# A decoder block on eight cores: packing the scattered transposes, re-ordering the first loads and groups, and moving work off the Vector engine

## The chip, the cores and the metric

The kernel runs on all eight NeuronCores of one Trainium2 chip, one sequence of 2048 tokens on each core, and the cores do not exchange data. The metric is device time in microseconds (us) of the slowest core. Most executions of a kernel agree within 0.3%. Now and then one die (cores 0 to 3 or 4 to 7) runs at a lower granted TensorE clock and the time is longer; such slow runs are left out wherever two kernels are compared.

The engines are called PE (matrix multiply), DVE (Vector), ACT (Scalar), POOL (GpSimd) and SP (which here only issues transfers). PEld is PE's weight load. "The kernel before" and "the changed kernel" are the two sides of the change. In the profiles `L453` and the like are line numbers of the kernel at hand; most instructions are issued by small helpers, so a line stands for a kind of instruction and not for a place in the algorithm, and the two kernels number the same helper differently.

## The reference, cut to what matters

```python
h = rmsnorm(x, norm_mix_g[l])
proj = h @ w_in[l]
q_pre, k_pre, v, o_pre, i_pre, f_pre, conf_in, gate_pre = jnp.split(proj, SPLITS, axis=-1)
# ... mLSTM branch on q, k, v: the "mixer loop" below ...

# Conformer convolution branch: this is the stretch ahead of the mixer loop
a, ga = jnp.split(conf_in, 2, axis=-1)
u = a * jax.nn.sigmoid(ga)
u = causal_dwconv(u, conf_conv_w[l], conf_conv_b[l])      # 31 taps, 1024 channels
u = jax.nn.silu(layernorm(u, conf_ln_g[l], conf_ln_b[l]))

x = x + (g_m * branch_m + g_c * branch_c) @ w_out[l]      # the w_out stage
x = x + (silu(f @ w_ffn_gate[l]) * (f @ w_ffn_up[l])) @ w_ffn_down[l]   # FFN, then down
gate = sigmoid(rmsnorm(x, norm_ple_g[l]) @ w_ple_gate[l]) # PLE gate weights
x = x + gate * (p[l] @ w_ple_proj[l])
```

D_MODEL is 1024, the sequence is cut into four token blocks T of 512 tokens (`TT`), each of four tiles of 128, and the 1024 convolution channels into eight groups c of 128.

## The kernel before

A small scheduler takes a program of operations in priority order, simulates it, fixes an order for each engine and inserts the semaphore waits. All SBUF data lie in one tensor, `arena`; `V(offset, n, dtype)` is a view of it. The parts that the change touches:

```python
def norm_pre(j):                                   # one tile of 128 tokens
    rms(xin0[j % 6], hb0[j % 3], gmix)             # ACT square sum, POOL pow, DVE multiply
    if j + 4 < NTOK:
        xload(j + 4)

def A(c, T):                                       # one projection group: u = a * sigmoid(ga)
    w = Aw[c % 4]                                  # four weight sets
    bg, ba = ringA(), ringA()
    mmg(bank(bg), [(w[:, 1, kc, :], hT[:, kc, tsl(T)]) for kc in range(8)])
    th = thr_()
    act(th, bank(bg), AF.Tanh, scale=0.5)
    mmg(bank(ba), [(w[:, 0, kc, :], hT[:, kc, tsl(T)]) for kc in range(8)])
    u = ur()
    stt(u, th, 1.0, bank(ba), ALU.add, ALU.mult)
    vtr(utr[c % 4][:, :, 1 + 16 * T:17 + 16 * T].rearrange("p c b -> p b c"),
        u.rearrange("p (b t) -> p b t", t=32))     # DVE 32x32 transposes, scattered bf16 output

def expand(h):                                     # filters into a block-diagonal weight
    i, half = h // 2, h % 2
    for q in range(4):
        # ... cut: src, dst: 32 partitions x 1024 elements ...
        ts('dve', dst, src, 0.5, ALU.mult)

def conv_evac(i):                                  # four PSUM transposes a convolution
    for T in range(NT):
        src = ps[:, 0:2048].rearrange("p (c b) -> p b c", b=64)[:, 16 * T:16 * T + 16, :]
        vtr(uc(i, T).rearrange("p (b t) -> p b t", t=32), src)

def stats(i, T):                                   # sums for the layer norm
    k = s2()
    b = pcol[:, PC_CCB + i:PC_CCB + i + 1]
    ts('dve', ucb[k], uc(i, T), b, ALU.add)
    act(usq[k], uc(i, T), AF.Square, bias=b)
    # ... cut: two matmuls ...

def ln_apply(i, T, b0):
    u = uc(i, T)
    stt(u, u, pcol[:, PC_CCB + i:PC_CCB + i + 1], bank(b0), ALU.add, ALU.mult)
    tt('pool' if i % 4 else 'dve', u, u, mrs, ALU.subtract)
    # ... cut: Silu on ACT ...
```

The loads at the start are issued at once: four x tiles, the gain, then A weights, two filter groups and gate weights. The order of work ahead of the mixer loop is: four norms; for each T three groups A(0..2, T); then A(3..7, T) with one convolution after every third group. At the other end, the last piece of the down weights:

```python
for n, T in forder:                                # FFN
    F(n, T)
    # ... cut ...
    if n == 9:
        cast('pg0', V(PGo[0], 4 * D, BF16), din['wPG'][:, 0:4 * D])
    if n == 18:
        cast('pg1', V(PGo[1], 2 * D, BF16), din['wPG'][:, 4 * D:6 * D])
    if n == 19:
        cast('pg2', V(PGo[2], 2 * D, BF16), din['wPG'][:, 6 * D:8 * D])
cast('dw3', V(dwoff[3], 4 * D, BF16), din['wD'][:, 18 * D:22 * D])   # over the FFN's thF buffers
```

## Time and profile before

| | kernel before |
|---|---|
| median of the 4 first runs | 1443.31 us (1439.45 to 1672.77; the largest was slow) |
| profiled run, slowest core | 1444.3 us (core 2) |
| first projection matmul | 40.6 us |
| mixer loop at full PE use from | about 340 us |
| last FFN matmul to last store of y | about 1192 to 1442 us |

Most of the lines that matter are shown in the prediction. One view that it used in words only is the list of transfers of the first 80 us (destination and source, issuing queue, number, size, median us from issue to landing), of the kernel before:

```profile
arena<-x SPq DMA_DIRECT2D x16, 512.0 KB, 16.4
arena<-wA POOLq DMA_DIRECT2D x4, 512.0 KB, 17.2
arena<-wS POOLq DMA_DIRECT2D x2, 1024.0 KB, 41.0
```

One tile of x takes 16.4 us to land with everything in flight together, among it two 1 MB pieces of q/k weights (wS) that nothing needs before about 250 us.

### The profile page before, as it was taken

What the parts mean: (1) busy time and instruction counts of PE and PEld (TensorE: products, weight loads), DVE (VectorE), ACT (ScalarE), POOL (GpSimd) and SP (SyncE); (2) the same over time, 40 slices, a digit from 0 to 9 for tenths busy, and PEclk for the clock granted to TensorE, in tenths of its full rate; (3) what the DMA queues carried; (4) which work ended last, traced back from release to release, by engine and by line L of the source; (5) the groups of instructions that cost most, each with busy time, mean ns of one, the idle gap of its engine ahead of it and who ended that gap; (6) DMA issues with size and microseconds to landing.
All of it is one profiled execution on the core that took longest, in us unless ns stands there. A gap on an engine that the chain in (4) does not pass through costs nothing.

```text
span 1444.3 us, 20115 instructions; the slowest of 8 cores (1428.2 to 1444.3 us)
## 1 busy us (share of the span) xinstructions
PE 1293.6 (90%) x6921; PEld 619.9 (43%) x7048; DVE 756.7 (52%) x1218; ACT 496.9 (34%) x917; POOL 277.4 (19%) x423
## 2 busy tenths in 40 slices
PE   0588999847989999999999999999999997999997
PEld 0234444314544454544444444444444443444443
DVE  4687899788888888621122255212121211545444
ACT  2332224666666666321111145111111110333233
POOL 2000001274445444322112201000000000000000
PEclk9888999768999999999999999999999998999999
DMA  9703231020033002332312498822212203121211
GB/s 196 188 28 60 48 55 31 0 44 1 1 59 59 2 1 45 74 74 31 57 30 40 75 254 222 154 37 37 44 30 44 44 16 102 59 88 59 88 59 73
DMA packets 22131, 94.23 MB, mean 65 GB/s; under 512 B 2704, under 2 KB 2832, under 8 KB 18960
## 3 DMA queue, kind: packets, MB, share of 16 engines
q0 software_dynamic: 9504, 48.26, 20.7%
q1 hardware_dynamic: 12528, 44.69, 9.3%
q8 instruction: 58, 0.95, 0.3%
q14 instruction: 41, 0.34, 0.1%
HBM read 124.41 MB, written 16.78 MB: 98 GB/s over the span
## 4 chain that ended last, share of the span: by engine, by line
PE 76%; DVE 7%; DMA 6%; issue 6%; ACT 4%; POOL 1%; SPq 0%; DVEq 0%; ACTq 0%; POOLq 0%
PE ps L396 74%; DVE arena L449 4%; DMA arena<-x 4%; ACT arena L419 3%; PE ps L399 2%; DVE arena L441 2%; DVE arena L446 1%; DMA arena<-wD 1%; ACT arena L435 1%; DMA x1d<-arena 1%; POOL arena L446 1%; DVE arena L453 0%; POOL arena L437 0%; SPq L84 0%; POOL arena L441 0%
## 5 line engine op out<-in xcount | busy, mean ns | idle before, releaser
L396 PE MATMUL ps<-arena 128*128 128x512 bf16 (+4 forms) x6281 | 1264.2, 357 | 74.9 <-ACT arena L419 23.4
L396 PEld LDWEIGHTS ps<-arena 128*128 128x128 bf16 (+1 forms) x6408 | 576.6, 99 | 720.8 <-issue 136.0
L419 ACT ACTIVATE arena<-ps 128x512 f32<-128x512 f32 (+3 forms) x414 | 217.4, 532 | 598.5 <-PE ps L396 580.6
L449 DVE SCALAR_TENSOR_TENSOR arena<-arena 128x512 f32<-128x512 bf16 (+3 forms) x353 | 278.0, 809 | 33.0 <-POOL arena L446 13.4
L449 DVE SCALAR_TENSOR_TENSOR arena<-arena,ps 128x512 f32<-128x512 f32 (+2 forms) x216 | 151.5, 709 | 211.7 <-PE ps L396 204.6
L446 POOL TENSOR_TENSOR arena<-arena 128x1 f32<-128x1 f32 (+3 forms) x152 | 139.7, 924 | 554.0 <-DVE arena L441 350.6
L419 ACT ACTIVATE arena<-arena 128x512 bf16<-128x512 f32 (+3 forms) x199 | 157.1, 800 | 244.1 <-DVE arena L446 95.5
L446 DVE TENSOR_TENSOR arena<-arena,ps 128x512 bf16<-128x512 f32 x88 | 60.5, 688 | 237.5 <-PE ps L396 235.9
L399 PE MATMUL ps<-arena 128*128 128x128 bf16 x640 | 60.5, 229 | 66.7 <-DVE arena L449 44.4
L399 PEld LDWEIGHTS ps<-arena 128*128 128x128 bf16 x640 | 47.3, 102 | 94.0 <-issue 76.6
L449 DVE SCALAR_TENSOR_TENSOR arena<-ps,arena 128x128 bf16<-128x128 f32 (+2 forms) x160 | 70.0, 466 | 32.2 <-DMA arena<-x 17.1
L435 ACT COPY arena<-ps 128x1024 bf16<-128x1024 bf16 (+1 forms) x72 | 59.0, 820 | 79.9 <-PE ps L399 79.5
L441 DVE TENSOR_SCALAR arena<-arena 32x1024 bf16<-32x1024 bf16 (+4 forms) x165 | 53.1, 327 | 57.8 <-ACT arena L419 55.8
L453 DVE STREAM_TRANSPOSE arena<-arena 128x512 bf16<-128x512 bf16 x32 | 78.7, 2458 | 1.3
L446 DVE TENSOR_TENSOR arena<-ps,arena 128x512 f32<-128x512 f32 (+2 forms) x34 | 23.1, 679 | 88.5 <-PE ps L396 85.3
L441 POOL TENSOR_SCALAR arena<-arena 128x514 bf16<-128x514 f32 (+1 forms) x61 | 54.0, 886 | 76.7 <-DVE arena L449 56.0
L437 POOL COPY arena<-arena 128x3 bf16<-128x3 bf16 x128 | 47.7, 375 | 106.3 <-ACT arena L419 64.4
L84 POOL DMA_DIRECT2D arena<-wF x22 | 11.8, 535 | 233.3 <-PE ps L396 233.3
L419 ACT ACTIVATE arena<-ps,arena 128x512 f32<-128x512 f32 x64 | 50.0, 783 | 0.0
L446 DVE TENSOR_TENSOR arena<-arena 128x2 f32<-128x2 f32 (+3 forms) x47 | 22.7, 492 | 15.7 <-ACT arena L419 15.6
L453 DVE STREAM_TRANSPOSE arena<-ps 128x512 f32<-128x512 f32 x32 | 23.6, 739 | 0.1
L435 ACT CAST arena<-ps 128x512 bf16<-128x512 f32 x32 | 18.8, 589 | 13.6 <-PE ps L396 12.4
(26 smaller groups left out, 104.6 us busy)
## 6 DMA issues: line engine op xcount, KB each, us to landing
arena<-x SPq DMA_DIRECT2D x32, 512.0 KB, 7.8
arena<-wF POOLq DMA_DIRECT2D x22, 512.0 KB, 5.3
arena<-wS POOLq DMA_DIRECT2D x8, 1024.0 KB, 10.0
arena<-wM POOLq DMA_DIRECT2D x8, 1024.0 KB, 10.3
x1d<-arena SPq DMA_DIRECT2D x16, 512.0 KB, 4.9
arena<-x1d SPq DMA_DIRECT2D x16, 512.0 KB, 4.3
y<-arena SPq DMA_DIRECT2D x16, 512.0 KB, 2.9
arena<-wD POOLq DMA_DIRECT2D x3, 1536.0 KB, 15.3
```

What stands on the lines that cost most here:

```text
L84: n.subs = [(lambda g: g.dma_start(out=out, in_=in_), [self.region(in_)], [self.region(out)])]
L396: S.op('pe', lambda e: e.matmul(out, lhsT=lhsT, rhs=rhs, start=start, stop=stop), [lhsT, rhs], [out], c)
L399: S.op('pe', lambda e: e.transpose(out=out, in_=in_, identity=identb), [in_, identb], [out], 0.06)
L419: S.op('act', lambda e: e.activation(out=out, in_=in_, func=func, **kw), [in_] + aps(bias, scale), [out] + aps(accum), c)
L435: S.op('act', lambda g: g.copy(out=out, in_=in_), [in_], [out], c)
L437: S.op(e, lambda g: g.tensor_copy(out=out, in_=in_), [in_], [out], c)
L441: S.op(e, lambda g: g.tensor_scalar(out=out, in0=in_, scalar1=s1, scalar2=s2, op0=op0, **kw), [in_] + aps(s1, s2), [out], vcost(e, out, [i ...
L446: S.op(e, lambda g: g.tensor_tensor(out=out, in0=a, in1=b, op=op), [a, b], [out], c)
L449: S.op('dve', lambda g: g.scalar_tensor_tensor(out=out, in0=a, scalar=s, in1=b, op0=op0, op1=op1), [a, b] + aps(s), [out], vcost('dve', ou ...
L453: S.op('dve', lambda g: g.transpose(out=out, in_=in_), [in_], [out], 0.19 + nfree(in_) * (1.0 if in_.dtype == F32 else 4.4) / 1e3)
```

## The change

The intent is to let PE start sooner and to take work off DVE in the stretch where both are full. It has seven parts: (1) u of T and T+2 are interleaved, so that one f32 transpose carries two bf16 values; (2) three of four filter expansions go to POOL; (3) the bias additions of the statistics go to ACT; (4) half of the layer-norm subtractions read the mean from PSUM on DVE, the other half stay on POOL; (5) x tiles, A weights and filters are one stream in order of need with at most three transfers in flight; (6) token block 0 is projected tile by tile, there are six A weight sets, and 24 of 32 groups run before the first convolution, in the order T = 0, 2, 1, 3 that the packing wants; (7) the last down weights load early and half of the PLE gate weights load late. The core of the diff:

```diff
+        TORD = (0, 2, 1, 3)
+        tiles = [4 * T + j for T in TORD for j in range(4)]
+        def stream(q, k, out, in_):
+            n = landed[0]
+            landed[0] += 1
+            dma(q, k, out, in_, dw=['st%d' % n], dr=['st%d' % (n - 3)] if n >= 3 else [])
 ...
-        def A(c, T):
-            w = Aw[c % 4]
+        def A(c, T, split=False):
+            w = Aw[c % 6]
+            u = uT[c if c < 6 else 2 * (c % 2) + T % 2]
 ...
+                if split:
+                    for j in range(4):
+                        mmg(bank(b, 128 * j, 128 * j + 128), [(w[:, m, kc, :], hT[:, kc, js(4 * T + j)]) for kc in range(8)])
 ...
-            stt(u, th, 1.0, bank(ba), ALU.add, ALU.mult)
-            vtr(utr[c % 4][:, :, 1 + 16 * T:17 + 16 * T].rearrange("p c b -> p b c"), u.rearrange("p (b t) -> p b t", t=32))
+            stt(u[:, T // 2::2], th, 1.0, bank(banks[1]), ALU.add, ALU.mult)
+            if T >= 2:
+                h = T % 2
+                vtr(utr4[c % 6][:, :, 1 + 16 * h:17 + 16 * h].rearrange("p c b -> p b c"), u.bitcast(F32).rearrange("p (b t) -> p b t", t=32), 4.6)
+                if h == 1:
+                    copy('dve', utr[c % 6][:, :, 0, 1], utr[c % 6][:, :, 32, 0])
 ...
-                ts('dve', dst, src, 0.5, ALU.mult)
+                if q == 0:
+                    ts('dve', dst, src, 0.5, ALU.mult)
+                else:
+                    ts('pool', dst, src, 0.5, ALU.mult, 1.0, ALU.mult)
 ...
-            ts('dve', ucb[k], uc(i, T), b, ALU.add)
+            act(ucb[k], uc(i, T), AF.Identity, bias=b)
 ...
-            tt('pool' if i % 4 else 'dve', u, u, mrs, ALU.subtract)
+            if i % 2:
+                tt('pool', u, u, mrs[T % 2], ALU.subtract)
+            else:
+                tt('dve', u, u, bank(b1), ALU.subtract)
 ...
                 if n == 9:
-                    cast('pg0', V(PGo[0], 4 * D, BF16), din['wPG'][:, 0:4 * D])
+                    cast('dw3', V(dwoff[3], 4 * D, BF16), din['wD'][:, 18 * D:22 * D])
 ...
-        cast('dw3', V(dwoff[3], 4 * D, BF16), din['wD'][:, 18 * D:22 * D])
+        cast('pg2', V(PGo[2], 4 * D, BF16), din['wPG'][:, 4 * D:8 * D])
```

Cut: the new buffer addresses, the scheduler's extra cost for table loads, a rule by which POOL waits for itself when it changes to other partitions, the new loops over groups and convolutions.

## The prediction

> **What bounds the kernel now.** I first read the fast runs (1445.6, 1441.0 and 1439.5 us; 1672.8 is the slow state) and the cores: 1428 to 1444 us, the two dies within 1%, so one core stands for all. Then the engines in nine stretches of the slowest core (length; busy us of PE, PEld, DVE, ACT, POOL; granted clock; DMA share; GB/s):
>
> ```profile
> 0.00:40.00 40.00, 5.06 (x40) 3.87 (x40) 19.18 (x23) 9.62 (x15) 9.67 (x29) 1.00 0.97 196
> 40.00:80.00 40.00, 24.48 (x114) 11.54 (x117) 25.31 (x33) 12.66 (x21) 3.74 (x7) 0.79 0.67 176
> 80.00:120.00 40.00, 32.86 (x168) 15.58 (x171) 32.33 (x31) 11.53 (x19) 4.35 (x8) 0.91 0.13 21
> 120.00:260.00 140.00, 128.54 (x1089) 62.12 (x1099) 127.51 (x191) 48.95 (x78) 8.56 (x23) 0.95 0.26 44
> 260.00:340.00 80.00, 46.88 (x163) 19.23 (x164) 64.33 (x90) 51.29 (x84) 45.25 (x46) 0.66 0.10 20
> 340.00:600.00 260.00, 240.88 (x1435) 128.47 (x1464) 226.11 (x456) 163.79 (x376) 115.42 (x189) 1.00 0.20 33
> 600.00:1190.00 590.00, 582.67 (x2781) 270.35 (x2836) 154.25 (x239) 128.17 (x217) 72.27 (x91) 1.00 0.36 73
> 1190.00:1210.00 20.00, 9.41 (x37) 3.90 (x37) 1.38 (x2) 0.60 (x1) 0.53 (x1) 0.73 0.72 184
> ```
>
> The kernel is PE-bound from 340 us on (PE 93 to 99%). The losses lie ahead of that: 50 us of idle PE in the first 80, 18 in 80 to 260, 33 in 260 to 340, and 10.6 at 1190. In 80 to 260 both PE and DVE are near full, so there no engine alone can give much. The pieces of the chain that ended last, from two stretches of it, name the two DMA waits (start, us, what):
>
> ```profile
> 5.23 32.98 DMA arena<-x
> ...
> 1193.50 13.31 DMA arena<-wD
> ```
>
> The first is x arriving beside everything else that was issued at the start; the first projection matmul runs at 40.6 us. The second is the last piece of the down weights, which overwrites a buffer that the FFN uses to its end. Who fills DVE in 80 to 260, by shape:
>
> ```profile
> L453 DVE STREAM_TRANSPOSE arena<-arena 128x512 bf16<-128x512 bf16 x29 | 71.3, 2457 | 1.0
> L453 DVE STREAM_TRANSPOSE arena<-ps 128x512 f32<-128x512 f32 x32 | 23.6, 739 | 0.1
> L441 DVE TENSOR_SCALAR arena<-arena 32x1024 bf16<-32x1024 bf16 x52 | 22.1, 425 | 0.7
> L449 DVE SCALAR_TENSOR_TENSOR arena<-arena,ps 128x512 bf16<-128x512 f32 x28 | 19.1, 681 | 12.1 <-PE ps L396 11.9
> L441 DVE TENSOR_SCALAR arena<-arena 128x512 bf16<-128x512 f32 x32 | 15.5, 492 | 0.7 <-PE ps L396 0.7
> ```
>
> The bf16 transposes alone are 71 of 160 busy us. In the layer-norm stretch, the timeline of DVE has this (start, us, instructions):
>
> ```profile
> 305.21 7.67 DVE L446 TENSOR_TENSOR arena<-arena 128x512 f32<-128x512 f32 x2
> ```
>
> Two subtractions of 0.69 us each (as at 275.57) take 3.8 us each while POOL does the same subtractions; PE idles meanwhile.
>
> [...]the transpose that scatters bf16 with a 130-byte step takes 2457 ns for 512 elements, the one with a dense output 739 ns.[...] the trace has 8 loads of 1283 ns, all before 340 us and mostly off the path.
>
> **The change part by part.**
> 1. Transposes: 32 bf16 ones become 16 f32 ones, each carrying tile T and T+2 interleaved. Same 512 elements, same scatter, so I keep 2.46 us each: 78.7 to 39.3 us, DVE -39.4. ([...]the multiply now writes bf16 with a step of two[...], so I leave it at 0.68.)
> 2. Filter expansion: 64 of 427 ns on DVE; 48 go to POOL. DVE -20.5. On POOL a one-input scale of 1024 elements took 1.04 us, so +50 us, plus waits on itself where the partition window changes.
> 3. Statistics: 32 bias additions of 492 ns go to ACT, at about the 0.74 us of the Square of that shape. DVE -15.5, ACT +24.
> 4. Layer norm: 24 subtractions on POOL (1.42 us) become 16; 8 on DVE (1.88 us[...]) become 16 from PSUM (0.69): 14.8 to 11.0 on DVE, about -11 on POOL.
> Sum on DVE: -39.4 - 20.5 - 15.5 - 3.8 = -79 us of the 269 it does before 340 us.
> 5. Loads: x and the A weights come as one stream in order of need, at most three in flight; filters and q/k weights wait. Up to the last x tile that is 8.4 MB of x, 0.5 of the gain, 3.1 of weights as stored, 12 MB; at the 176 to 196 GB/s above, 61 to 68 us, so x ends near 70 us, as it about does now. What is gained is the first tile: four transfers of 0.26 to 0.5 MB share the pipe, x lands near 7 us, and the norm chain (1.06 + 0.18 + 0.15 + 0.55 + 1.28, PE transposes 1.0, copy 0.7 to 1.0, hops) ends near 14 us.
> 6. Splitting tile 0 into 128-column matmuls lets PE start on one token tile. It is nearly free: 8 such transposes took 0.45 us in the chain, 56 ns each, 4 x 56 = 224 ns against about 216 for one 512-column matmul.
> 7. Order: six A weight sets and u-buffers instead of four; 24 of 32 A groups run before the first convolution; the transposes no longer stand just ahead of each convolution.
> 8. The last down weights load early, into space of their own; the late load is half of the PLE gate weights, of 1 MB, which took 13.3 us for the down piece and is needed only about 19 us after the down stage starts (its first gate matmuls come after two down tiles). I count the 10.5 us as gained.
>
> **Adding up the stages.** PE work at full clock: an A group is 16 x 0.216 = 3.46 us[...].
> - First: 24 groups and 128 transposes, 83 + 7 = 90 us, at the clock of about 0.9 seen from 80 to 120, 100 us: 14 to 114. DVE needs about 85 in it and x has landed by 70, so PE sets it.
> - Second: 8 groups 27.7,[...] statistics 48 x 0.216 = 10.4, gates 4: 66, with clock and hand-offs (a convolution waits for four PSUM transposes of 0.74 before it) 74: to 188. DVE needs 44, ACT about 45, POOL 37 to 45.
> - Third: two convolutions, four q/k groups, the rest of the statistics: PE 18, ACT 20, DVE 16; 22: to 210.
> - Fourth: the layer norm, where PE waits on DVE. DVE had 64 busy of 80; now 60, with the 16 of idling cut to about 7: 67, to 277.
> The same point is now reached at 340, so -63; with the down weights -11: 1443 - 74 = 1369.
>
> **The rivals.** (a) PE alone bounds all of it from 14 us on: its 239 busy us before 340, some at a low clock, are about 222 at full; the point would be reached near 240, the kernel at 1335. For it: 79 us off DVE. Against: the norm still needs over 40 us of DVE after the last statistics. (b) POOL becomes the bound of the convolutions: three expansions a half are 3.2 us by row, but if partition-window waits[...] make it 2 us each, 6 us a half, 96 us for 16 halves, more than the 74 + 22 of stages two and three, and the kernel would lose 10 to 25 of the gain: 1380 to 1395. For it: POOL also issues the filter loads in the same order, behind waits. (c) The stream starves: three in flight with a round of waits between, at say 130 GB/s, x would end near 95 us and stage one near 125, +10 to 15. (d) f32 scatter costs more than bf16 scatter, say 4 us: +24 us of DVE, but half of that lies where PE sets the pace: +10. (e) The freed time returns as waits in the mixer loop at 340 to 600, where DVE has 226 of 260: the loop is unchanged, so I give this little.
>
> **Range and chances.** The gain has four parts of about 27 (start), 15 (80 to 260), 20 (norm) and 11. Rivals b, c, d together take perhaps 30 and a adds 35. I put 1368 in the middle and 1338 to 1400 for 8 in 10. Within 2% begins at 1414, which needs two rivals at once: 0.06; faster 0.93; slower 0.01.
>
> **What would show it.** First projection matmul near 14 us (10 to 18) instead of 40.6; x waits in the chain short. Scattered transposes: 16 of about 2.5 us. DVE busy up to the mixer loop about 190 us. The mixer loop's first full-PE stretch near 277 us instead of 340. POOL expansions near 1.05 us. Subtractions on DVE at 0.69 us. No wait on down weights and none over 3 us on the gate weights. Wrong would be: PE idle under POOL in the convolutions, a granted clock still near 0.7 in the norm with idle as before, or a difference after 340 us other than the 11.

The sum came to 74 us: 63 ahead of the mixer loop and 11 in the tail. A term within it is cut above: 23.4 us for six convolutions, part of the 66 of the second stage (two more convolutions are in the 18 of PE of the third). It rested on a rate for narrow matmuls that no trace shows; in the kernel before, 64 matmuls of 64 columns, one convolution, take PE 2.1 to 2.5 us of busy time. The 0.216 us of a 512-column matmul is in the chain of the kernel before (32 in 6.92 us from 47.01). That an f32 element of the scatter costs what a bf16 one does (2.46 us for 512), that the interleaved multiply stays at 0.68 us, and that subtractions from PSUM take 0.69 us beside POOL's were estimates from the times above.

## The result, and the profile after

The changed kernel took 1378.27 us in the median of ten runs (fast ones 1376.96 to 1381.05, their mean 1378.4); the kernel before, with more runs beside it, 1444.91 us in the median of sixteen. The ratio of the two is 0.953, with a 95% interval of 0.9495 to 0.9566. Ratios are the mean time of one kernel's fast runs over that of the other's of the same rounds, so not quite the ratio of these medians. The profiled executions are 1444.3 and 1377.7 us: 66.6 us less, where 75 were predicted. Seven of the sixteen runs of the kernel before are slow ones or ones of 1456 to 1462 us; the other nine have a mean of 1442.4 us, and against them the gain is 64 us.

The engines of the changed kernel in stretches of time (length; busy us of PE, PEld, DVE, ACT, POOL; granted clock; DMA share; GB/s). The first four are those of the same view before; the mixer loop, which began at 340, now begins near 291, so the next stretches end 40 to 60 us sooner:

```profile
0.00:40.00 40.00, 16.88 (x220) 16.20 (x221) 19.35 (x23) 10.15 (x15) 11.34 (x25) 1.00 0.78 157
40.00:80.00 40.00, 28.67 (x249) 18.53 (x250) 19.85 (x29) 15.40 (x27) 7.65 (x14) 0.79 0.64 150
80.00:120.00 40.00, 38.43 (x259) 20.89 (x262) 22.20 (x29) 12.14 (x19) 18.27 (x21) 1.00 0.27 41
120.00:260.00 140.00, 126.50 (x1073) 61.58 (x1082) 97.04 (x160) 94.08 (x152) 73.81 (x92) 0.98 0.38 65
260.00:300.00 40.00, 23.91 (x127) 11.52 (x128) 37.86 (x66) 24.95 (x50) 21.54 (x26) 0.83 0.14 27
300.00:600.00 300.00, 279.10 (x1630) 146.98 (x1662) 233.76 (x476) 167.90 (x388) 126.87 (x194) 1.00 0.18 36
1130.00:1150.00 20.00, 19.89 (x92) 9.07 (x93) 2.06 (x3) 1.67 (x3) 0.53 (x1) 1.00 0.45 94
```

These are of core 4, the slowest of the profiled run. Up to 60 us it is not typical: PE is busy 25.7 us there, and 28.4 to 29.3 on the other seven cores, so the text below gives the range of all cores where it matters. PE has 16.88 us of the first 40 where it had 5.06. DVE fell from 127.5 to 97.0 of the 140 us from 120 on, ACT and POOL took over (49 to 94 and 9 to 74). The changed kernel is further along at 260 us than the kernel before (its layer norm starts near 224), so part of this is other work in the same window. The end of the FFN (1130 to 1150, before it 1190 to 1210) has no hole, and its clock is 1.00 where it was 0.73.

Who fills DVE in the first 300 us of the changed kernel (line, operation, output and input with their shape, number; busy us, mean ns; idle ahead of it):

```profile
L466 DVE STREAM_TRANSPOSE arena<-ps 128x512 f32<-128x512 f32 x32 | 21.0, 683 | 0.0
L466 DVE STREAM_TRANSPOSE arena<-arena 128x512 f32<-128x512 f32 x16 | 17.8, 1110 | 1.0
L459 DVE TENSOR_TENSOR arena<-arena,ps 128x512 f32<-128x512 f32 x16 | 10.6, 680 | 0.0
L450 DVE COPY arena<-arena 128x32 bf16<-128x32 bf16 x8 | 3.6, 451 | 0.1
```

The scattered transposes went from 32 of 2458 ns to 16 of 1110 ns, 78.7 to 17.8 us, and the PSUM subtractions take 680 ns. The same view of POOL has the moved expansions:

```profile
L454 POOL TENSOR_SCALAR arena<-arena 32x1024 bf16<-32x1024 bf16 x48 | 54.1, 1127 | 19.4 <-PE ps L408 13.1 <-POOL arena L454 5.4 <-DVE arena L763 0.4
```

Here "POOL arena L454 5.4" is POOL waiting for itself, 5.4 us in all. And the start, from the chain that ended last (start us, us, what):

```profile
1.99 3.69 POOL arena L633
...
6.45 10.30 DMA arena<-wA
16.81 7.93 DMA arena<-x
...
27.01 1.86 PE ps L408 x16
...
55.70 4.50 PE ps L408 x11
```

L408 is the line of the matmul helper; here these are projections. The weights of the first group are issued only at 6.45 us, behind a POOL instruction of 3.69 us, and an x tile that the next work stands behind lands at 24.7 us. The second token block's projections begin at 55.70. The last two are core 4's own: on the other seven cores the group at 27.01 begins at 23.7 us and the second block at 50.8 to 51.9 us. The first projection is at 19.4 us on all eight.

To find where the 66.6 us came from I set equal events of both traces side by side (core 2 before, core 4 after, us):

| event | before | after | gained so far |
|---|---|---|---|
| issue of `gh` (end of the layer norm's projections) | 297.8 | 250.4 | 47.4 |
| first w_out weights | 460.3 | 410.9 | 49.4 |
| first store of x1 (w_out stage starts) | 824.5 | 775.2 | 49.3 |
| last store of x1 | 891.4 | 837.2 | 54.2 |
| first reload of x1 (end of the FFN) | 1192.4 | 1138.7 | 53.7 |
| last store of y | 1441.6 | 1375.1 | 66.5 |

On these two cores 49 us are gained ahead of the mixer loop, none in it, 5 in the w_out stage and 13 after the FFN. But the same events can be read on all eight cores. From the first to the last store of x1 the kernel before took 61.9 to 66.9 us (mean 63.6; core 2 had the longest) and the changed kernel 61.7 to 64.3 (mean 62.8). So the 5 us are mostly the scatter of the cores, and about 1 us is left. The mean gains over the eight cores are 50.7 us ahead of the mixer loop (up to the issue of `gh`), none from there to the first store of x1, 0.9 in the w_out stage, none in the FFN and 11.8 after it (247.8 to 236.0 us from the first reload of x1 to the last store of y): 63.1 us in all.

### The profile page after: what moved, and what is told of

It reads as the page before. It is cut to its first block, busy times and chain, and to the rows that moved or that the text cites. A ratio compares the mean times of both kernels' runs of the same rounds, so it can differ in the third digit from the quotient of the medians.

```text
span 1377.7 us, 20871 instructions; the slowest of 8 cores (1372.4 to 1377.7 us)
## 1 busy us (share of the span) xinstructions
PE 1275.6 (93%) x7209; PEld 630.0 (46%) x7336; DVE 673.7 (49%) x1140; ACT 510.8 (37%) x947; POOL 337.0 (24%) x479
## 4 chain that ended last, share of the span: by engine, by line
PE 80%; ACT 5%; issue 5%; DVE 4%; DMA 3%; POOL 3%; ACTq 0%; SPq 0%; DVEq 0%; POOLq 0%
PE ps L408 78%; ACT arena L432 4%; DVE arena L462 3%; PE ps L411 2%; DMA arena<-x 1%; DMA arena<-x1d 1%; POOL arena L459 1%; ACT arena L448 1%; POOL arena L450 1%; DMA arena<-wA 1%; DVE arena L459 1%; POOL arena L454 0%; POOL arena L633 0%; ACT L432 0%; DVE arena L466 0%
## 5 line engine op out<-in xcount | busy, mean ns | idle before, releaser
L408 PE MATMUL ps<-arena 128*128 128x512 bf16 (+6 forms) x6569 | 1247.0, 346 | 54.2 <-ACT arena L432 19.7
L408 PEld LDWEIGHTS ps<-arena 128*128 128x128 bf16 (+1 forms) x6696 | 587.3, 99 | 672.4 <-issue 88.5
L459 POOL TENSOR_TENSOR arena<-arena 128x1 f32<-128x1 f32 (+3 forms) x144 | 128.8, 896 | 517.7 <-DVE arena L454 325.8
L432 ACT ACTIVATE arena<-arena 128x512 bf16<-128x512 f32 (+3 forms) x231 | 174.9, 787 | 187.0 <-DVE arena L459 76.6
L459 DVE TENSOR_TENSOR arena<-arena,ps 128x512 bf16<-128x512 f32 (+1 forms) x104 | 71.1, 686 | 237.9 <-PE ps L408 236.2
L454 POOL TENSOR_SCALAR arena<-arena 128x514 bf16<-128x514 f32 (+2 forms) x109 | 111.6, 1024 | 106.6 <-DVE arena L462 64.8
L462 DVE SCALAR_TENSOR_TENSOR arena<-ps,arena 128x256 bf16<-128x256 f32 (+2 forms) x160 | 69.7, 465 | 23.4 <-DMA arena<-x 8.8
L85 POOL DMA_DIRECT2D arena<-wF x22 | 11.7, 533 | 231.7 <-PE ps L408 231.7
L459 DVE TENSOR_TENSOR arena<-ps,arena 128x512 f32<-128x512 f32 (+2 forms) x34 | 22.9, 678 | 76.4 <-PE ps L408 61.1
L454 DVE TENSOR_SCALAR arena<-arena 128x1 f32<-128x1 f32 (+3 forms) x85 | 20.1, 242 | 62.8 <-ACT arena L432 52.7
L454 DVE TENSOR_SCALAR arena<-ps,arena 128x256 bf16<-128x256 bf16 x64 | 20.7, 340 | 0.0
L466 DVE STREAM_TRANSPOSE arena<-arena 128x512 f32<-128x512 f32 x16 | 17.8, 1110 | 1.0
```

Source lines behind the costliest of these rows:

```text
L85: n.subs = [(lambda g: g.dma_start(out=out, in_=in_), [self.region(in_)], [self.region(out)])]
L408: S.op('pe', lambda e: e.matmul(out, lhsT=lhsT, rhs=rhs, start=start, stop=stop), [lhsT, rhs], [out], c)
L432: S.op('act', lambda e: e.activation(out=out, in_=in_, func=func, **kw), [in_] + aps(bias, scale), [out] + aps(accum), c, t)
L454: S.op(e, lambda g: g.tensor_scalar(out=out, in0=in_, scalar1=s1, scalar2=s2, op0=op0, **kw), [in_] + aps(s1, s2), [out], vcost(e, out, [i ...
L459: S.op(e, lambda g: g.tensor_tensor(out=out, in0=a, in1=b, op=op), [a, b], [out], c)
L462: S.op('dve', lambda g: g.scalar_tensor_tensor(out=out, in0=a, scalar=s, in1=b, op0=op0, op1=op1), [a, b] + aps(s), [out], vcost('dve', ou ...
```

## The experiments

Twelve kernels ran. "Mean" is that of the fast runs; the changed kernel's own is 1378.4 us. The means of the kernel before in the three calls were 1445.6, 1444.3 and 1442.2 us. The first two contain one run each (1457.31 and 1459.09 us): its cores 4 and 5 had a clock of 0.946 to 0.948 against 0.962 to 0.968 of the others. Without these two runs the means are 1442.7, 1441.4 and 1442.2 us, so there is no drift. Gains over the kernel before are given against these means.

### 1. Packing undone

```diff
-            stt(u[:, T // 2::2], th, 1.0, bank(banks[1]), ALU.add, ALU.mult)
-            if T >= 2:
-                vtr(utr4[c % 6][...], u.bitcast(F32)..., 4.6)
+            u = u[:, TT * (T // 2):TT * (T // 2) + TT]
+            stt(u, th, 1.0, bank(banks[1]), ALU.add, ALU.mult)
+            vtr(utr[c % 6][:, :, 1 + 16 * h:17 + 16 * h, T // 2]..., u..., 4.4)   # bf16, step of 132 bytes
```

> The changed kernel with the packing of the transposes undone: 32 bf16 transposes of 512 elements again, each into every second column of the same buffer, [...]with a step of 132 bytes instead of 130. Theory (the price is that of a 2-byte scattered write): 2.4 to 2.5 us each, DVE busy +61 us before the mixer loop; DVE would then be nearly full in the first 24 groups (86 us of work in the 75 us from 60 on), so 1388 to 1400 us. Rival 1 (the price came from the 130-byte step, which is not a whole number of 4-byte words): about 1.1 us each, DVE +18 us, and the time stays within 4 us of 1378. Rival 2 (packing is idle because PE sets the pace): 2.45 us each but the time still within 4 us of 1378.

Mean 1389.3 us (1390.1, 1389.5, 1388.4), ratio 0.9609: 11 us slower than the changed kernel. DVE's transposes by shape:

```profile
L466 DVE STREAM_TRANSPOSE arena<-arena 128x512 bf16<-128x512 bf16 x32 | 78.6, 2467 | 1.8
```

The step is now 132 bytes, as in the packed form, and the price is what it was with 130 bytes (2458 ns). A transpose of 512 elements written 132 bytes apart costs 2467 ns if they have two bytes and 1110 ns if they have four. So the scatter alone does not set the price, as I had assumed when I kept 2.46 us for both; the element width does. Whether it does so in the scattered write or in the transposition of two-byte elements itself no run tells, since none has a bf16 transpose with a dense output; the 739 ns that the prediction set beside the 2457 were of f32 from PSUM, so it compared two widths. The 61 us of DVE that packing saves are worth 11 us of time here. That much of that DVE time lay where PE was the bound, or could be filled otherwise, is my reading of the stages; no run shows it.

### 2. Expansion back on DVE

```diff
-                if q == 0:
-                    ts('dve', dst, src, 0.5, ALU.mult)
-                else:
-                    ts('pool', dst, src, 0.5, ALU.mult, 1.0, ALU.mult)
+                ts('dve', dst, src, 0.5, ALU.mult)
```

> The changed kernel with the filter expansion back on DVE alone (64 instructions of about 0.43 us there, none of 1.13 us on POOL). Theory (DVE had to be relieved in the convolutions): DVE +18 us, POOL -54 us, 2 to 6 us slower than 1378. Rival (POOL sets the pace of the convolutions after the change): faster, 1370 to 1376, with the idle time of PE in 135 to 205 gone.

Mean 1382.8 us (1382.4, 1383.2, 1382.7), ratio 0.9563: 4 us slower. All 64 are on DVE at 421 ns. POOL was no bound in the changed kernel, and the move is worth a fifth of the 20 us that it takes off DVE.

### 3. Bias additions back on DVE

```diff
-            act(ucb[k], uc(i, T), AF.Identity, bias=b)
+            ts('dve', ucb[k], uc(i, T), b, ALU.add)
```

> The changed kernel with the 32 bias additions of the statistics back on DVE. Theory (after the change ACT is what PE waits for from 200 to 245 us, where it is busy 16 to 18.5 of 20 us, and DVE has room since its transposes take 1.1 us): 2 to 8 us faster than 1378, ACT busy about 22 us less. Rival (DVE still needs the relief): 2 to 6 us slower.

Only two of its six runs were fast, 1381.4 and 1380.35 us, so no ratio is given: some 2.5 us slower. I had expected that ACT is the bound in the third stretch (it has 15.8 to 18.5 us of 20 busy there) and that giving work back to DVE would gain; that was wrong. On DVE the addition takes 720 ns now, not the 492 of the kernel before. In kernel 4, where no expansion runs on POOL, it takes 481 ns. The expansions left on DVE show the same: 561 ns each in the changed kernel, beside those of POOL, and 421 to 430 ns in kernels 2 and 4. So a likely reason is that DVE is slower while POOL expands; no run isolates it.

### 4. All four reliefs undone together

Edits 1, 2, 3 and 5 in one kernel.

> The changed kernel with all four reliefs of DVE undone together (packing, expansion, statistics, subtraction from PSUM), but its loads, order, split and late-stage loads kept. Theory (the gain before the mixer loop is mostly DVE relief): DVE busy +70 to +95 us before the mixer loop, 1410 to 1430 us. Rival (the order of loads and groups does most of it, PE being near full anyway): 1380 to 1395 us.

Mean 1408.8 us (1408.4 to 1409.3), ratio 0.9743: 30.4 us slower. Alone they cost 11 + 4 + 2.5 + 0, in sum under 18 us. DVE's busy time in the first 300 us is 199 to 249 us in these kernels: 243 with packing undone, 203 and 215 with expansion or additions, 199 with the subtractions, 249 with all. Each alone falls into room that the other three made; that reading fits the sum but no run isolates it.

### 5. Layer-norm subtractions as before

```diff
-            if i % 2:
-                tt('pool', u, u, mrs[T % 2], ALU.subtract)
-            else:
-                tt('dve', u, u, bank(b1), ALU.subtract)
+            tt('pool' if i % 4 else 'dve', u, u, mrs[T % 2], ALU.subtract)
```

> The changed kernel with the subtractions of the layer norm as before: 24 on POOL, 8 on DVE, all with the mean row in SBUF. Theory[...]: the DVE subtractions go from 0.68 to about 1.9 us and PE idles longer from 230 to 290 us; 6 to 12 us slower than 1378. Rival (DVE work in the norm is not what sets the pace): within 3 us.

Mean 1378.1 us, ratio 0.9539: no difference. DVE's and POOL's subtractions in it:

```profile
L459 DVE TENSOR_TENSOR arena<-arena 128x512 f32<-128x512 f32 x8 | 13.2, 1659 | 0.0
L459 POOL TENSOR_TENSOR arena<-arena 128x512 f32<-128x512 f32 x24 | 32.6, 1391 | 4.4 <-DVE arena L462 4.3
```

With the mean row in SBUF, one subtraction on DVE takes 1659 ns in the mean, where it takes 680 with the mean row read from PSUM, yet 13.2 us against 10.6 of DVE is a small difference once the rest of the stretch is lighter. That these subtractions would be slower I had right (about 1.9 us expected); it was worth nothing in time, and why they are slower no run isolates.

### 6. Early down weights alone, on the kernel before

The down part of the diff above, with the buffers that it needs, on the kernel before.

> The kernel before with part 8 alone: the last down weights early, half of the gate weights late. Theory: the wait of PE on the down weights (10.5 us) goes and with it the low clock after it, so 11 to 13 us off 1444: 1431 to 1434, with no wait on the gate weights. Rival (the late gate weights take the place): 4 to 8 us off. The mixer loop's entry does not move.

The four runs were 1445.1, 1447.2, 1431.5 and 1444.1 us (ratio 0.9981, 0.9896 to 1.0065). I call them unclear, because in three of them a pair of cores ran at a lower clock. In the profiled one die 0 had 1420.5 to 1427.6 us, and cores 6 and 7 had 1444.0 and 1438.9 at a clock of 0.952 and 0.951. Repeated with five rounds:

> The same kernel as dw_alone again, because three of its four runs were in the slow state: the kernel before with early down weights and late gate weights. From its tail in the trace (13.5 us shorter than before's): fast runs at 1429 to 1433. If the gain at the tail is partly given back elsewhere: 1434 to 1440. Rival (hidden anyway): 1441 to 1446.

The three undisturbed runs are 1432.1, 1433.2 and 1431.7 us, against a mean of 1442.2 for the kernel before: 9.8 us faster. (A fourth, 1444.1: its cores 0 and 1 had a clock of 0.951 against 0.966 to 0.971 of the others, and by the trace 0.76 to 0.81 of it between 120 and 260 us; with it the ratio is 0.9951.) The stretch of the old hole, on core 3:

```profile
1180.00:1190.00 10.00, 10.00 (x49) 4.52 (x47) 1.38 (x2) 0.00 (x0) 0.53 (x1) 1.00 0.96 268
1190.00:1210.00 20.00, 20.00 (x106) 9.57 (x105) 5.64 (x8) 4.22 (x6) 1.11 (x2) 1.00 0.18 51
```

PE is busy throughout at full clock, where it had 9.41 of 20 us at 0.73. This part holds alone. (The tail, from the first reload of x1 to the last store of y, takes 235.7 us on every core of both traces of this kernel and 246.4 to 249.2 us, mean 247.8, in the kernel before. That is 12 us shorter; the difference to the 9.8 us by the times of the slowest core is not explained.)

### 7. The zeroings of the filter buffers after the first norms

Three DVE instructions zero the block-diagonal buffers at the start, 3.47 us each, ahead of the first norm.

```diff
-        for i in range(3):
-            memset('dve', V(BD[i], 4096, BF16), 0.0)
+            if k == 4:      # after the fifth projection group, held there by a read of a norm's output
+                # the same three zeroings
```

> The changed kernel with the three zeroings of the filter blocks (3.47 us each on DVE) moved behind the first norms. In the changed kernel they hold the norm of tile 0 on DVE until 14.6 us although its square sum is there at 8.0, and one of them keeps POOL's 3.69 us instruction and with it the first A weights back to 6.4 us. Theory: first PE transposes near 11 us instead of 17.3, A weights issued near 3 us; x of the second and third tile still sets the rest, so 2 to 6 us off 1378. Rival (all of it is hidden behind the arrival of x and the weights): within 1.5 us.

Mean 1378.6 us (1379.4, 1377.5, 1378.7), ratio 0.9539: no difference, though the start moved. PE's first transposes ran at 9.94 us instead of 17.32, and the first weights were issued at 3.06 us instead of 6.45. The POOL instruction that held up the first weights, in the changed kernel and then in this one (timeline: start, us, instruction):

```profile
1.99 3.69 POOL L633 TENSOR_SCALAR_AFFINE_SELECT arena<-arena 128x128 f32<-128x128 f32 x1
```

```profile
2.00 0.29 POOL L633 TENSOR_SCALAR_AFFINE_SELECT arena<-arena 128x128 f32<-128x128 f32 x1
```

In the changed kernel a DVE zeroing of 3.47 us started in the same moment (1.99 us), and POOL's instruction ended just after it. Where did the early start go? The zeroings are only moved, not removed: on all eight cores they now run on DVE between about 46 and 63 us (on core 0 at 48.41, 52.69 and 57.52 us, 3.47 us each), in front of the third block's norms. PE then waits 1.9 us for those norms on all eight cores, and not at all in the changed kernel. From 60 to 140 us PE is busy 76.1 to 76.7 us at a clock of 0.96 to 0.98, where seven cores of the changed kernel have 78.6 (core 4: 78.2) at 1.00. Up to 60 us PE has 29.4 to 32.8 us, against 28.4 to 29.3 on seven cores of the changed kernel. So the moved zeroings give back what the early start gained, and this run does not show that an early start is worth nothing. Kernels 8 and 9 carry the same late zeroings.

### 8. A faster front

```diff
+        # x and A loads issued ahead of POOL's set-up work; zeroings late as in 7
-            dma(q, k, out, in_, dw=['st%d' % n], dr=['st%d' % (n - 3)] if n >= 3 else [])
+            dma(q, k, out, in_, dw=['st%d' % n], dr=['st%d' % (n - 6)] if n >= 6 else [])
-            transpose8(trb(), hb0[n % 3], hT[:, :, js(tiles[n])], 'act' if n % 2 else 'dve')
+            transpose8(trb(), hb0[n % 3], hT[:, :, js(tiles[n])], 'act' if n % 2 and n > 3 else 'dve')
```

> The changed kernel with four edits at the start: the zeroings late, the first weight loads issued ahead of POOL's set-up, six transfers of the stream in flight instead of three, and the copies of the first four tiles on DVE. Theory (the start was 13 us later than I predicted because of instruction order on DVE, ACT and POOL and the window of three): projections start near 13 us and the first tile group ends near 30 instead of 40; 6 to 12 us off 1378, so 1366 to 1372. Rival (the stream sets the pace of the first 75 us, so an earlier start is given back as waits for x): 1375 or more.

Mean 1381.6 us, ratio 0.9562: 3 us slower. Two waits of its first 60 us (engine and line waited for: us in total, times, longest):

```profile
POOL arena L85 <- DMA arena<-wA: 11.3, 2, 8.9
DVE arena L462 <- POOL arena L459: 11.0, 4, 8.5
```

L85 is a transfer issued by POOL. It waits on POOL for an earlier transfer to land, and behind it stands the norm's power (L459) that DVE waits for. First transposes 17.52 us on the core shown (14.1 to 17.5 over the eight), where the changed kernel has 17.3 on all. The second block starts at 53.1 to 57.7 us, later than the 50.8 to 51.9 of seven cores of the changed kernel, which fits the loss of 3 us.

### 9. Six in flight, without the rest of 8

```diff
+        # zeroings late as in 7
-            dma(q, k, out, in_, dw=['st%d' % n], dr=['st%d' % (n - 3)] if n >= 3 else [])
+            dma(q, k, out, in_, dw=['st%d' % n], dr=['st%d' % (n - 6)] if n >= 6 else [])
```

> The changed kernel with the zeroings moved late (worth 0 by itself) and six transfers in flight instead of three. If three in flight starve the stream (157 GB/s in the first 40 us where the kernel before had 196), the second token block lands 4 to 8 us earlier and the kernel gains 3 to 8 us: 1370 to 1375. Rival: the first tile shares the pipe with five others and lands later, and the projections of block 0 cover it anyway: within 2 us of 1378.

Mean 1382.9 us (1381.7 to 1383.6), ratio 0.9587: 4.5 us slower than the changed kernel and 4.4 than kernel 7, from which it differs by the number in flight alone; by the gain over the kernel before (59.3 us, where kernel 7 gained 62.8) it is 3.5. Both theory and rival missed. The profiled run fell in the slow state on die 0, so this is core 5 of the undisturbed die; a projection of the second block:

```profile
48.90 11.37 PE L408 MATMUL ps<-arena 128*128 128x512 bf16 x43 [1.25 <-ACT arena L448]
```

The second block starts at 47.3 to 51.7 us over the eight cores (mean 49.3), hardly before kernel 7 (mean 49.7) and about 2 us before seven cores of the changed kernel. The first 40 us moved some 181 GB/s instead of 157. But PE then waited for norms of the third block between 76 and 81 us (2.8 and 1.4 us, 4.1 in all on each core, against 1.9 in kernel 7), while POOL ran seven expansions of 1.0 to 1.8 us between 67 and 80 us. Two of the norm multiplies on DVE took 3.38 and 3.75 us beside POOL's expansions, 2.46 to 2.47 in kernel 7. From 60 to 140 us PE was busy 73.9 to 74.5 us, against 76.1 to 76.7. Three in flight was the better setting. These waits are of the size of the loss; that they are its cause is my reading.

### 10. Without the split of token block 0

```diff
-            A(c, T, split=(T == 0))
+            A(c, T)
```

> The changed kernel, token block 0 with whole 512-column matmuls instead of four 128-column ones: PE can't start before the fourth tile is through the norm. Theory (the split is what turns the early first tile into a gain): first projection near 38 us instead of 19, +5 to +12 us: 1383 to 1390. Rival: block 2's tiles land at about 55 us anyway and PE waits for them, and there are six weight sets of block 0 work only for three sets landed by then, so the 14 us of PE work of block 0 fits between: +0 to +4.

Mean 1382.3 us (1381.4 to 1384.0), ratio 0.9584: 4 us slower, and also by the gain over the kernel before (59.9 us against 64). PE's first projection in it:

```profile
30.50 12.58 PE L408 MATMUL ps<-arena 128*128 128x512 bf16 x48 [1.25 <-ACT arena L448]
```

It starts 11 us later than at 19.39, runs through in one piece, and then PE waits for the second block, whose projections start at 55.23 us (53.5 to 55.4 over the eight cores, some 3 us later than on seven cores of the changed kernel). The split is worth about 4 us; of the 11 us of the first projection the wait for the second block's tiles hides most.

### 11. The loads alone, on the kernel before

The stream with three in flight, x and A weights in order of need, filters and gate weights held until two token blocks are through; everything else as before.

```diff
+            stream('sp', 'x%d' % (j % 6), xin0[j % 6], din['x'][js(j), :])
 ...
-        load_A(1)
-        load_A(2)
-        load_cw(0)
-        cast('wif', ...)
-        load_A(3)
-        load_cw(1)
+            if T == 2:      # ahead of the groups of the third block
+                # load_A(3), filters, gate weights and the first expansions
```

> The kernel before with only the loads changed: x tiles and A weights as one stream in order of need, at most three in flight, filters, gate weights and the fourth A weight held until two token blocks are through. Transposes, POOL, order of groups and tail as before. My theory now: the 48 us gained ahead of the mixer loop is mostly engine work taken off DVE plus the order, and the loads give the start alone: first projection matmul near 20 to 25 us instead of 40.6, but with four weight sets and DVE at 2.46 us a transpose the 80 to 260 us stretch is as full as it was, so of some 17 us at the start 8 to 15 are kept: 1428 to 1436. Rival 1: nothing is kept, DVE's work before the mixer loop bounds it: 1441 to 1447. Rival 2: the loads carry most of the rest: 1410 to 1425.

Mean 1440.0 us (1438.8 to 1440.7), ratio 0.9983 (0.9969 to 0.9998): 2 us. My theory (8 to 15 us) failed and the rival that nothing is kept was nearly right. The timeline of its PE:

```profile
17.05 1.01 PE L399 MATMUL ps<-arena 128*128 128x128 bf16 x8 [17.05 <-DVE arena L449]
...
42.27 12.62 PE L396 MATMUL ps<-arena 128*128 128x512 bf16 x48 [1.25 <-ACT arena L435]
```

x lands in 5.2 us instead of 16.4, and the first transposes run at 17 us instead of 26. But a 512-column projection needs four tiles, and the fourth is through its norm only at 41 us, so the first projection is at 42.27 us, later than before. And the stretch from 120 to 260 us is as full as it was: PE 129.7, DVE 127.3 of 140. By this reading an earlier first tile is worth something only with the split, and only when the rest is lighter.

### What is left

Of about 64 us, the four reliefs carry 30.4 when all are undone on the changed kernel, and the down weights 9.8 when done alone on the kernel before. The other 24 or so belong to the split (4 on the changed kernel), the loads (2 on the kernel before) and the order of the groups with six weight sets. This last part was not undone alone, since the packed transposes need the order 0, 2, 1, 3; what it carries is what is left over and is not shown, and the parts need not add up. No variant beat the changed kernel.

## Why the prediction was right or wrong

The time was predicted at 1368 (1338 to 1400) and came out at 1378; "faster" was right with 0.93. The sum was 74 us and the parts came out, in the mean of the eight cores, at 51 ahead of the mixer loop (predicted 63), 1 in the w_out stage (predicted none) and 12 in the tail (predicted 11). By its own steps:

1. **Transposes.** "16 of about 2.5 us" was mis-sized: 16 of 1.110 us. The premise that an element of the scatter keeps its price when it is twice as wide fell in experiment 1. The error was in the change's favour: 17.8 us of DVE instead of 39.3. The eight column copies, which the sum left out, were 451 ns each.
2. **Expansion.** POOL took 1127 ns (predicted 1.05 us) and its self-waits came to 5.4 us. Rival b (POOL becomes the bound) is ruled out: back on DVE the kernel is slower.
3. **Statistics.** ACT's instructions of this shape take 728 ns, as predicted from the Square. It is a gain of 2.5 us, smaller than its 15.5 us on DVE.
4. **Layer norm.** The PSUM subtractions take 680 ns, as predicted, and with the mean row in SBUF one takes 1659 ns (experiment 5). But in the finished kernel this is worth 0; the "20 (norm)" of the range was not due to it. The stretch did shorten to 67 us as predicted, with a DVE that is still full (37.9 of 40 us).
5. **Start.** This is the step that failed. First projection at 19.4 us instead of 14, with only 16 matmuls; the next at 27.0 (23.7 on the other seven cores). Two things were overlooked in the first 8 us: the 3.47 us zeroings stand ahead of the first norm on DVE, and beside one of them a POOL instruction takes 3.69 us (0.29 us when it was moved, experiment 7), behind which the first weights are issued. Then PE waits for the norms of the second block, from about 41 to 55 us on the core shown and to 51 or 52 on the others: of the 20 us from 40 to 60 it is busy 8.8, on the others 11.7 to 12.4. I had PE setting the pace from 14 us on with x landed by 70.
6. **Split.** Its cost was well sized where PE runs without a gap (128 matmuls of 128 columns in 7.16 us from 33.27, 56 ns each; the 16 at 27.01 took 1.86), and it is worth about 4 us.
7. **Stages.** The first stage ends near 133 us instead of 114; the second takes 72 us (predicted 74, the cut term in it), the third 19 (22), the fourth 67 (67), to 291 instead of 277. (On the other seven cores the first convolution starts at 130.4 to 131.6 us.) So the first stage is the whole of the shortfall, 16 to 21 us by core. PE's own work in it was well sized: from 14 to 133 us it is busy 97 to 101 of 119 us, near the 100 of the sum. The other 18 to 22 us are PE standing idle for the late start, for the norms of single tiles and for the second block, and the sum had no such term. Removing one of these waits did not gain: with the zeroings moved, the first projection is 5 to 7 us sooner (12.1 to 14.2 us), but the zeroings then stand ahead of the third block's norms (experiment 7). A start that is earlier at no cost elsewhere was not run, so what it would be worth stays open.
8. **Tail.** 11 us were predicted, 9.8 measured alone by the times, 12 between the traces in the mean of the eight cores. No wait of PE on the gate weights appears.

DVE has 188 us up to the mixer loop (291 us), where 190 were predicted. That is in part luck: the transposes came out 21.5 us cheaper than in the sum, so other parts must have been dearer. The expansions left on DVE (561 ns), the copies (451) and the interleaved writes (729 instead of 682) are only about 6 us of that; the rest was not traced. Of the rivals, c (the stream starves) was seen in part: the first 40 us move 157 GB/s instead of 196. But six in flight, which moved more, was no faster. Rival a (PE alone from 14 us on) did not come, rival d fell with experiment 1, and rival e (waits in the mixer loop) did not come either: the loop took as long as before.

## What to carry to other kernels

Before carrying the price of a strided write over to another element width, run it with that width: two bf16 values carried as one f32 more than quartered the scattered transposes (78.7 to 17.8 us). Moves between engines need not add up: undo them one by one and together (here 11, 4, 2.5 and 0 us alone, 30.4 together). An early first tile was worth only 2 us while the first matmul still waited for four tiles; cut the matmul too, and look for what stands ahead of a transfer on the queue that issues it. Read a gain of a few us on all cores before explaining it: the 5 us between two cores in the w_out stage were 1 us in the mean of eight.
